# In attention, the scores of the next unit are multiplied ahead of the transposes of the last unit's probabilities

## Chip, cores and metric

The kernel runs on one core of one Trainium2 chip, in one launch. The metric is the device time of that launch in microseconds (us); smaller is better. The median of three runs before the change is 1122.41 us (1121.69 to 1124.14).

## The reference

One layer of an encoder trunk over 1024 tokens of width 1024, all in float32: a norm, one input projection whose columns feed a pooling mixer and attention, an output projection with residual, a gated MLP with a causal convolution, a gated per-layer embedding, and a final norm. The change lies in attention alone:

```python
q, k, v = jnp.split(z[..., POOL_W:], 3, axis=-1)     # 8 heads of 64
...
# chunk_attention: each chunk of 64 tokens attends to itself and the 8 chunks before it
s = jnp.einsum('bqhd,bkhd->bhqk', qb, kb) * scale + bias   # clipped relative position, per head
s = jnp.where(valid, s, -jnp.inf)
pr = jax.nn.softmax(s, axis=-1)
out = jnp.einsum('bhqk,bkhd->bqhd', pr, vb)
```

## The kernel before

The engines go by their short names: PE multiplies matrices, ACT and DVE work elementwise, POOL does a few elementwise pieces, SP issues transfers. Matrices are held as two parts, a high one rounded to float32r and a low one that holds the remainder, and a product is three matmuls (`mm3`, L136 to L138). So whatever is made elementwise and multiplied later is split by two instructions: a copy of the high part on ACT and a subtraction on DVE.

**Units.** The 1024 tokens are 8 query tiles of 128. Attention works on pairs of heads, `c` = 0 to 3, and in each on 6 units: unit 0 holds query tiles 0, 1 and 2, units 1 to 5 hold tiles 3 to 7, one each. There are 24 units (`NU`), and 25 visits `unit(u)`. A visit multiplies the scores of unit `u`, and takes the probabilities of unit `u - 1`, whose softmax was made in the visit before, one step on. A query tile looks at up to 5 key tiles (`BANDT`).

**A visit on PE.** PE's order is the order of the program (`manual_schedule`), and so is that of ACT and DVE in this stretch. In a visit, PE runs

- `probs_t(u - 1)` (L421): the probabilities of the last unit, two heads, are transposed by PE in pieces of 64 by 64, four per key tile of the unit, so 16 to 24 matmuls. The first 8 pieces of 64 columns go to banks 2 and 3 of PSUM (called near here), those of a fifth key tile and on to the last columns of banks 6 and 7 (far);
- `scores(u)` (L398): 12 matmuls for one query tile, 18 for unit 0 of a head pair. The two heads run side by side, each on 64 rows of the array. Head 0 writes bank 4, then 6, head 1 bank 5, then 7;
- matmuls of the projections that are still to be done (`fill`, a generator: q and k of the next head pairs, then the pooling mixer's columns), 12 to 27 of them, alternating between banks 0 and 1;
- in three of six visits, `values(u - 1)` (L473): the products of probabilities and v, for a group of query tiles (0 to 2, 3 to 5, or 6 and 7) whose last unit was just transposed. They go to bank 5 and the free one of banks 0 and 1, or, for the group of two tiles, both heads into one bank. ACT copies half of each result to `otmp` (L476) and DVE adds it to the other half (L479).

**A visit on ACT and DVE.** Their instructions are put into a list with due times (`push`) and issued in order of those when the visit calls `flush()`, which is after its projection matmuls have been issued. The list of a visit holds

- of the transposed probabilities: ACT's copies (L439) and DVE's remainders (L441), near ones ahead of far ones. The transposes of the next visit write the same banks again;
- of the softmax of the new scores: DVE adds the bias and takes the minimum (`least`, L363 for four and five key tiles, L367 for fewer), from PSUM to `Sb`; ACT's exponential with its sum (L375); DVE's reciprocal (L378); the scaling, by DVE for head 0 (L373) and by ACT for head 1 (L371). `Sb` has one buffer per head, which the transposes read;
- the copies of finished projections (L279 for q and k, L559 for the mixer) and the splits of q and k (L308 to L312) and of weights (L502, L504).

The lines of the change stand in `unit`, L671 and L673:

```python
            if u:
                probs_out(probs_t(u - 1), valued[0])
            if u < NU:
                softmax(scores(u), valued[0])
```

`probs_t` and `scores` issue PE's matmuls at once; `probs_out` and `softmax` only push ACT's and DVE's instructions.

Of the kernel before, what the change touches and what calls it, by code (L numbers as in the profile page):

```python
# [75 lines left out]
NU = len(UNITS)  # L76
# [8 lines left out]
def group_at(t):  # L85

    return next(g for g in GROUPS if g[0] <= t < g[1])


def is_last(u):  # L90

    t = UNITS[u][1][-1]
    return t + 1 == group_at(t)[1]
# [8 lines left out]
def trunk(tc, xT, pT, vecs, w_qk0, w_in, w_v, bias, counts, pool_w, w_out, w_up, w_down,  # L102
# [4 lines left out]
    with tc.tile_pool(name="sb", bufs=1) as sb, \  # L107
# [176 lines left out]
        def push(t, *fns):  # L284

            for n, fn in enumerate(fns):
                pending.append((t + 0.8 * n, len(pending), fn))

        def flush():
            todo = sorted(pending, key=lambda p: p[:2])  # L290
            pending.clear()
            owed.clear()
            for _, _, fn in todo:
                fn()
# [51 lines left out]
        def load_bias(h):  # L346
            b = biasb[h % 3]
            sp.dma_start(b, bias[h])

            def turned():  # L350
                act.activation(b, b, AF.Copy, scale=-1.0)
                pool.memset(b[0:64, 576:640], BIG)
                pool.memset(b[64:128, 0:64], BIG)
            return turned

        def softmax(todo, valued):

            for i, (x, b, ps, S, s_) in enumerate(todo):
                z = 2 * i / len(todo)

                def least(b=b, ps=ps, S=S, s_=s_):
                    if len(ps.shape) == 3:
                        dve.tensor_tensor_reduce(  # L363
                            S.rearrange("p (a b) -> p a b", a=2), ps,
                            b.rearrange("p (a b) -> p a b", a=2), 1.0, BIG, ALU.add, ALU.min, s_[:, 0:1])
                    else:
                        dve.tensor_tensor_reduce(S, ps, b, 1.0, BIG, ALU.add, ALU.min, s_[:, 0:1])  # L367

                def scaled(x=x, S=S, s_=s_):
                    if x:  # L370
                        act.activation(S, S, AF.Copy, scale=s_[:, 2:3])  # L371
                    else:
                        dve.tensor_scalar(S, S, s_[:, 2:3], None, ALU.mult)  # L373
                push(1.0 + 0.8 * z, least)
                push(1.9 + 0.85 * z, lambda S=S, s_=s_: act.activation(  # L375
                    S, S, AF.Exp, bias=s_[:, 0:1], scale=-1.0, accum_out=s_[:, 1:2]))
                ready = max(2.95 + 0.01 * z, 1.91 + 0.85 * z) if valued else 2.95 + 0.55 * z
                push(ready, lambda s_=s_: dve.reciprocal(s_[:, 2:3], s_[:, 1:2]))  # L378
                push(3.9 + 0.1 * z if x else max(ready + 0.005, 3.0 + (0.01 if valued else 0.55) * z), scaled)
# [4 lines left out]
        def scores(u):  # L384

            c, ts = UNITS[u]
            Kh, Kl = K[c % 2]
            todo = []
            for z, t in enumerate(ts):
                ki, nk = max(0, t - 4) * P, min(t + 1, BANDT)  # L390
                n = nk * P
                wide = n // 2 if nk > 3 else max(n, 256)
                off, place = (0, 1, 3)[z] * P, ((0, 0), (0, 256), (1, 0))[z]
                places = [[4 + x + 2 * (place[0] + y) for y in range(2 if nk > 3 else 1)] for x in range(2)]
                for i, (q, k) in enumerate(((Q[0], Kh), (Q[0], Kl), (Q[1], Kh))):
                    for y in range(len(places[0])):
                        for x in range(2):
                            pe.matmul(PS[:, places[x][y], place[1]:place[1] + wide], q[halves[x], t * P:(t + 1) * P],  # L398
                                      k[halves[x], ki + y * wide:ki + (y + 1) * wide], start=i == 0, stop=i == 2,
                                      tile_position=(HD * x, 0))  # L400
                for x in range(2):
                    p0 = places[x][0]
                    ps = PS[:, p0:p0 + 3:2, 0:wide] if nk > 3 else PS[:, p0, place[1]:place[1] + n]
                    todo.append((x, biasb[(2 * c + x) % 3][:, 640 - n:640], ps, Sb[x][:, off:off + n], st[nstat[0] % 8]))
                    nstat[0] += 1
            return todo

        def probs_t(u):

            c, ts = UNITS[u]  # L410
            total = key_tiles(u)

            def place(x, m):
                n = 2 * m + x
                return (2, HD * n) if n < 8 else (6, 512 + HD * (n - 2 * total))

            for x in range(2):
                for m in range(total):
                    bank, col = place(x, m)
                    for y in range(2):  # L420
                        pe.transpose(PS[:, bank + y, col:col + HD], Sb[x][halves[y], m * P:(m + 1) * P],  # L421
                                     ident[halves[y], halves[y]], tile_position=(HD * y, 0))
            todo, m = [], 0
            for t in ts:
                nk = min(t + 1, BANDT)
                b0 = block_at(t + 1 - nk, t)
                for a, b in ((0, min(nk, 4 - m)), (max(4 - m, 0), nk)):
                    if b > a:
                        bank, col = place(0, m + a)
                        todo.append((b0 + a, b0 + b, bank, PS[:, bank:bank + 2, col:col + 2 * HD * (b - a)]))  # L430
                m += nk
            return todo

        def probs_out(todo, valued):
            for a, b, bank, ps in todo:
                src = ps.rearrange("p a (n q) -> p n a q", q=HD)
                hi, lo = [pt[:, a:b].rearrange("p k x (a q) -> p (k x) a q", a=2) for pt in PT]
                far = bank > 3
                push(3.5 if far else 0.0, lambda hi=hi, src=src: act.activation(hi, src, AF.Copy))  # L439
                push((3.55 if valued else 4.4) if far else 2.5 if valued else 3.7,  # L440
                     lambda lo=lo, src=src, hi=hi: dve.tensor_tensor(lo, src, rv(hi), ALU.subtract))  # L441

        credit, turns, valued = 0.0, [], [False]
# [203 lines left out]
        def lay_due(u):  # L647

            for c, x, h in list(qk_ready):
                if u >= (c - 1) * PER + (0 if x else PER - 1 if h else 1):  # L650
                    qk_ready.remove((c, x, h))
                    push(max(4.8, now[0] + 0.4), *lay(c, x, h))
# [4 lines left out]
        def unit(u):  # L657

            nonlocal credit
            now[0] = 0.0  # L660
            unit_at[0] = u
            if u < NU:
                c, ts = UNITS[u]
                for h in range(2 if ts[-1] > 3 else 1):
                    while not all((c, x, h) in laid for x in range(2)):
                        next(fill)
                        lay_due(u - 1)
                        flush()
            valued[0] = u > 0 and is_last(u - 1)
            if u:  # L670
                probs_out(probs_t(u - 1), valued[0])  # L671
            if u < NU:
                softmax(scores(u), valued[0])  # L673
                if u % PER == PER - 1:
                    for h in (2 * c + 3, 2 * c + 4):
                        if h < N_HEADS:
                            push(3.0, lambda h=h: turns.append(load_bias(h)))
                lay_due(u)
                credit += ROOM[u % PER]
                now[0] = 1.25  # L680
                least = LEAST[u % PER] if u else 0
                while credit >= 1 or least > 0:
                    if valued[0] and credit < 2 and least < 1 and 4.7 < at[0] < 5.4:
                        break
                    now[0] += STEP
                    credit -= 1
                    least -= 1
                    if next(fill, True) is False:
                        break
                    lay_due(u)  # L690
            else:
                for _ in range(DRAIN):
                    now[0] += STEP
                    next(fill)
            flush()
            if u:
                values(u - 1)
            if turns and (u % PER == PER - 1 or u % PER == 1):
                turns.pop(0)()
            run_later(LATER)  # L700
# [765 lines left out]
```

## Time and profile before

| | before |
|---|---|
| median of 3 runs | 1122.41 us (1121.69 to 1124.14) |
| the profiled execution, its own time | 1122.08 us |
| its span, first to last instruction | 1120.3 us |
| TensorE clock granted (mean) | 0.998 |
| PE busy | 1108.7 us, 99% |
| DVE busy | 850.7 us, 76% |
| ACT busy | 581.7 us, 52% |
| POOL busy | 167.9 us, 15% |
| first scores in the trace | 74.3 us |
| last transposes in the trace | 248.7 to 250.2 us |

How to read it: the profiled execution is one run; its time holds the span and 1.8 us around it. Busy time of PE is the union of its matmuls, whose ends are modelled and which overlap in the pipeline, so a short pause between two matmuls can hide in it; starts of matmuls tell more than their ends. Lines such as L421 are lines of the kernel; a group that a helper issues has the helper's line. In rows of the timeline stand the start, the duration, engine, line, operation, tiles written and read, shapes, and the count of merged instructions; in brackets how long the engine had been idle and what released it.

### The profile page before, as it was taken

How to read it: one execution, taken by the hardware profiler on the slowest of the kernel's cores; microseconds unless marked ns; L12 is line 12 of the kernel's file. 1: busy time of each engine (PE TensorE's matmuls, PEld its weight loads, DVE VectorE, ACT ScalarE, POOL GpSimd, SP SyncE). 2: the span in 40 equal slices, each digit the busy share in tenths (PEclk: the TensorE clock that was granted, in tenths of full speed). 3: DMA queues.
4: the chain of work that ended last, by engine and by line, in shares of the span. 5: the costliest groups of instructions: out<-in, count | busy, mean ns of one | idle time of the engine just before them, and what ended most of it. 6: DMA issues, size and time to landing. Idle time of an engine off the chain costs nothing.

```text
span 1120.3 us, 15614 instructions
## 1 busy us (share of the span) xinstructions
PE 1108.7 (99%) x5674; PEld 921.3 (82%) x5674; DVE 850.7 (76%) x1438; ACT 581.7 (52%) x1006; POOL 167.9 (15%) x212
## 2 busy tenths in 40 slices
PE   9999999999999999999999999999999999999997
PEld 7888888888888888888888888888888888888887
DVE  7537777778578878887787878777877789986845
ACT  8336777765665545443443444344544444674634
POOL 0000101186013200220121012201120112000000
PEclk9999999999999999999999999999999999999999
DMA  8100111104600452764567456756575556420003
GB/s 308 50 1 20 62 43 39 51 16 136 197 29 1 109 155 95 164 156 140 150 160 168 133 160 151 172 138 160 142 174 145 137 156 140 132 94 20 1 34 117
DMA packets 64878, 124.83 MB, mean 111 GB/s; under 512 B 7329, under 2 KB 8737, under 8 KB 64801
## 3 DMA queue, kind: packets, MB, share of 16 engines
q1 hardware_dynamic: 50688, 98.33, 26.8%
q0 software_dynamic: 13824, 25.17, 14.2%
q8 instruction: 44, 0.72, 0.3%
q10 hardware_dynamic: 288, 0.33, 0.1%
q14 instruction: 34, 0.27, 0.1%
HBM read 109.13 MB, written 14.68 MB: 111 GB/s over the span
## 4 chain that ended last, share of the span: by engine, by line
PE 65%; DVE 3%; issue 2%; ACT 1%; POOL 1%; POOLq 0%; DVEq 0%; ACTq 0%
PE PS L136 21%; PE PS L137 21%; PE PS L138 21%; DVE R L142 1%; ACT R L141 1%; POOL TB L925 0%; POOL F L915 0%; DVE F L907 0%; DVE F L1191 0%; ACT TB L896 0%; PE PS L778 0%; POOL small L782 0%; ACT F L770 0%; DVE TB L918 0%; DVE TB L919 0%
## 5 line engine op out<-in xcount | busy, mean ns | idle before, releaser
L136 PE MATMUL PS<-R 128*128 128x512 f32 (+1 forms) x1088 | 422.2, 388 | 0.2
L137 PE MATMUL PS<-R 128*128 128x512 f32 (+1 forms) x1088 | 418.7, 385 | 0.0
L138 PE MATMUL PS<-R 128*128 128x512 f32 (+1 forms) x1088 | 418.5, 385 | 0.0
L136 PEld LDWEIGHTS PS<-R 128*128 128x128 f32 x1088 | 204.6, 188 | 44.6 <-issue 2.9
L138 PEld LDWEIGHTS PS<-R 128*128 128x128 f32 x1088 | 204.5, 188 | 41.3
L137 PEld LDWEIGHTS PS<-R 128*128 128x128 f32 x1088 | 204.6, 188 | 39.8 <-DVE R L249 0.2
L141 ACT ACTIVATE R<-F 128x512 fp32r<-128x512 f32 (+2 forms) x221 | 137.4, 636 | 177.1 <-PE PS L137 85.6
L142 DVE TENSOR_TENSOR R<-F,R 128x512 fp32r<-128x512 f32 (+2 forms) x221 | 154.5, 713 | 49.7 <-ACT R L141 49.0
L1160 DVE TENSOR_TENSOR F<-F,PS 128x512 f32<-128x512 f32 x140 | 92.6, 681 | 6.8 <-PE PS L138 6.5
L850 DVE TENSOR_TENSOR F<-F 128x512 f32<-128x512 f32 x88 | 60.5, 688 | 44.8 <-DMA F<-in_w_up 42.1
L141 ACT ACTIVATE BQ<-RW 128x512 fp32r<-128x512 f32 x90 | 52.6, 622 | 80.4 <-PE PS L137 76.3
L1103 POOL DMA_DIRECT2D RW<-Yd x56 | 49.5, 889 | 264.4 <-DMA RW<-Yd 200.8
L1103 POOL DMA_DIRECT2D RW<-in_w_down x40 | 36.5, 966 | 228.7 <-DMA RW<-in_w_down 191.1
L142 DVE TENSOR_TENSOR BQ<-RW,BQ 128x512 fp32r<-128x512 f32 x90 | 59.1, 684 | 2.6 <-PE PS L137 2.2
L137 PE MATMUL PS<-BQ 128*128 128x512 f32 x140 | 54.6, 390 | 0.1
L136 PE MATMUL PS<-R,BQ 128*128 128x512 f32 x140 | 54.5, 389 | 0.0
L138 PE MATMUL PS<-R,BQ 128*128 128x512 f32 x140 | 54.5, 389 | 0.0
L136 PE MATMUL PS<-BQ 128*128 128x512 f32 x140 | 54.5, 389 | 0.0
L137 PE MATMUL PS<-R,BQ 128*128 128x512 f32 x140 | 54.5, 389 | 0.0
L138 PE MATMUL PS<-BQ 128*128 128x512 f32 x140 | 54.5, 389 | 0.0
L986 ACT ACTIVATE F<-F,vec 128x1024 f32<-128x1024 f32 (+1 forms) x25 | 28.6, 1143 | 44.1 <-DVE F L961 41.9
L375 ACT ACTIVATE F<-F,small 128x640 f32<-128x640 f32 (+4 forms) x64 | 44.0, 689 | 14.0 <-DVE small L363 12.6
(177 smaller groups left out, 1589.7 us busy)
## 6 DMA issues: line engine op xcount, KB each, us to landing
F<-in_w_up SPq DMA_DIRECT2D x91, 256.0 KB, 4.3
RW<-Yd SPq DMA_DIRECT2D x60, 256.0 KB, 3.8
RW<-Yd POOLq DMA_DIRECT2D x56, 256.0 KB, 4.9
RW<-in_w_down SPq DMA_DIRECT2D x50, 256.0 KB, 2.9
RW<-in_w_down POOLq DMA_DIRECT2D x40, 256.0 KB, 6.6
Yd<-F SPq DMA_DIRECT2D x40, 256.0 KB, 3.1
F<-in_w_in SPq DMA_DIRECT2D x10, 512.0 KB, 3.5
F<-in_xT SPq DMA_DIRECT2D x16, 256.0 KB, 5.4
```

The costliest lines, as they stand in the source:

```text
L136: pe.matmul(ps, ahi, bhi, start=first, stop=False, skip_group_check=more)
L137: pe.matmul(ps, ahi, blo, start=False, stop=False, skip_group_check=more)
L138: pe.matmul(ps, alo, bhi, start=False, stop=last, skip_group_check=more)
L141: both = (act.activation(hi, src, AF.Copy), dve.tensor_tensor(lo, src, rv(hi), ALU.subtract))
L142: dve.tensor_tensor(lo, src, rv(hi), ALU.subtract))
L375: push(1.9 + 0.85 * z, lambda S=S, s_=s_: act.activation(S, S, AF.Exp, bias=s_[:, 0:1], scale=-1.0, accum_out=s_[:, 1:2]))
L850: return dve.tensor_tensor(rawu[to], rawu[a], rawu[b], op)
L986: act.activation(y, Gb[:, 2 + a:2 + b], AF.Identity, bias=vec[:, C_CB + fi:C_CB + fi + 1], scale=cw(2))
L1103: pool.dma_start(t, src, accum_op=ALU.add)
L1160: dve.tensor_tensor(t, t, PS[:, 4 + d], ALU.subtract if n in (1, 5) else ALU.add)
```

## The change

In a visit, `scores(u)` is called, and so its matmuls are issued on PE, before `probs_t(u - 1)`; the list of scores is handed to `softmax` afterwards. The calls of `push` keep their order and their due times, so that the order of ACT's and DVE's instructions is the same.

```diff
             valued[0] = u > 0 and is_last(u - 1)
+            todo = scores(u) if u < NU else []
             if u:
                 probs_out(probs_t(u - 1), valued[0])
             if u < NU:
-                softmax(scores(u), valued[0])
+                softmax(todo, valued[0])
                 if u % PER == PER - 1:
```

Visit 0 has no probabilities to transpose and visit 24 no scores to multiply; the order on PE changes in the other 23.

## The prediction

> **What bounds the kernel now.** I read the page first: its part 1 shows TensorE (PE) at 99% of the span, so time moves only where PE stands still or where its own instructions take longer.
>
> ```profile
> span 1120.3 us, 15614 instructions
> PE   1108.7 (99%) x5674; PEld 921.3 (82%) x5674; DVE 850.7 (76%) x1438; ACT 581.7 (52%) x1006; POOL 167.9 (15%) x212
> ```
>
> Then the windows view of attention, 80 to 256 us, and PE's waits there (who waited for whom: total, times, longest).
>
> ```profile
> 80.00:256.00 176.00, 172.85 (x1416) 144.30 (x1416) 131.51 (x318) 125.33 (x258) 45.44 (x67) 1.00 0.14 42
> ...
> PE PS L473 <- DVE B L441: 1.8, 4, 0.8
> PE PS L421 <- DVE B L441: 0.8, 2, 0.5
> PE PS L473 <- ACT B L439: 0.5, 1, 0.5
> ```
>
> PE is idle 176.00 - 172.85 = 3.15 us there, and only 0.8 of it stands ahead of the transposes (L421), where the scores could go first. So there is little to win; what the change can cost must be looked for in one visit. The timeline of one whole visit (start, duration):
>
> ```profile
> 98.01 1.53 DVE L441 TENSOR_TENSOR B<-PS,B 128x1024 fp32r<-128x1024 f32 x2
> ...
> 99.19 0.39 PE L138 MATMUL PS<-R 128*128 128x512 f32 x1
> ...
> 99.51 0.84 PE L421 MATMUL PS<-ident,F 64*128 64x64 f32 x20
> ...
> 100.16 1.13 PE L398 MATMUL PS<-R 64*128 64x320 f32 x12
> 100.33 1.03 ACT L439 ACTIVATE B<-PS 128x1024 fp32r<-128x1024 f32 x1 [0.84 <-PE PS L421]
> ...
> 101.22 0.50 PE L136 MATMUL PS<-R,B 128*128 128x512 f32 x1
> 101.32 0.82 DVE L363 CUSTOM_DVE_ANT_0 F<-PS,F 128x640 f32<-128x640 f32 x1 [1.77 <-PE PS L398]
> ...
> 102.19 0.83 ACT L375 ACTIVATE F<-F,small 128x640 f32<-128x640 f32 x1 [0.83 <-DVE small L363]
> ...
> 103.83 0.36 ACT L439 ACTIVATE B<-PS 128x256 fp32r<-128x256 f32 x1
> ...
> 104.06 1.33 PE L473 MATMUL PS<-B,R 128*128 128x384 f32 x7
> ...
> 105.20 0.42 DVE L441 TENSOR_TENSOR B<-PS,B 128x256 fp32r<-128x256 f32 x1
> ...
> 105.68 0.55 PE L473 MATMUL PS<-B,R 128*128 128x128 f32 x2 [0.29 <-DVE B L441]
> ```
>
> Read it thus. Transposes T (L421) run 99.51 to 100.16, scores S (L398) to 101.22, then projection matmuls, then the values V (L473). ACT copies what T made, first the near part (1024 wide, banks 2 and 3), starting 0.17 after T's end; DVE starts its minimum over the scores (L363) 0.10 after S's end; the exponential (L375) starts 0.05 after that minimum. V stops at its eighth matmul until DVE's far remainder (105.20 + 0.42 = 105.62) is there: 105.68, 0.06 later.
>
> **The change part by part.** Nothing is added or removed; in 23 visits (units 1 to 23) 12 or 18 score matmuls with their weight loads pass 16 to 24 transposes on PE. No DMA is issued by the moved step, and no order written out for ACT or DVE changes; SP's and POOL's queues are not passed.
>
> *Borders between kinds of matmul.* A projection to T costs 99.51 - 99.19 = 0.32. The other borders:
>
> ```profile
> 73.96 0.39 PE L138 MATMUL PS<-B,R 128*128 128x512 f32 x1
> 74.28 1.50 PE L398 MATMUL PS<-R 64*128 64x256 f32 x18
> 75.71 0.50 PE L136 MATMUL PS<-R 128*128 128x512 f32 x1
> ...
> 205.34 0.84 PE L421 MATMUL PS<-ident,F 64*128 64x64 f32 x20
> 205.99 1.48 PE L398 MATMUL PS<-R 64*128 64x256 f32 x18
> 207.40 0.50 PE L136 MATMUL PS<-R 128*128 128x512 f32 x1
> ...
> 249.65 0.59 PE L421 MATMUL PS<-ident,F 64*128 64x64 f32 x12 [0.46 <-DVE B L441]
> 250.17 0.50 PE L136 MATMUL PS<-R 128*128 128x512 f32 x1
> ```
>
> A projection to S costs the same 0.32 (74.28 - 73.96). Eighteen scores take 1.43 behind a projection and 1.41 behind T: +0.02. T costs 0.65 / 20 = 0.033 each ahead of S, so 12 would be 0.39; ahead of a projection they took 0.52: +0.13 at most. S, no longer ahead of a projection, gives something back, which no row of before shows: between nothing and twice that 0.11 net (0.22). Per visit -0.09 to +0.13, over 23 visits -2.1 to +3.0 us. I take **0**: the same three borders (wide to narrow, narrow to narrow, narrow to wide) stand in every visit, only the names differ.
>
> *A. The wait that is new.* V of the group of query tiles 0 to 2 puts its first half in bank 5; S writes bank 5 with its second matmul. Before, T stood between.
>
> ```profile
> 131.79 0.55 DVE L479 TENSOR_TENSOR F<-PS,F 64x384 f32<-64x384 f32 x1 [0.34 <-ACT F L476]
> 131.94 0.71 PE L421 MATMUL PS<-ident,F 64*128 64x64 f32 x16
> ```
>
> S would start at 131.94, but DVE reads bank 5 until 132.34; with 0.06 to pass it on, 0.46 of wait. The second pair's weights load meanwhile, so that it can follow closer than the 0.18 that a pair takes on average (1.06 / 6); I put 0.1 on that: 0.35 a time, in 4 head pairs **+1.4** (1.3, or 1.8 with nothing given back). This is late next on PE, and what queues behind it is T, and so the near copies.
>
> *How finely waits are told apart.* S writes banks 4 to 7; T's far part lies at the end of banks 6 and 7, in other columns. Does a wait go by bank or by column? Two rows of a V whose halves share one bank:
>
> ```profile
> 124.45 0.77 ACT L476 ACTIVATE F<-PS 64x256 f32<-64x256 f32 x2 [1.27 <-PE PS L473]
> ...
> 125.25 0.42 DVE L479 TENSOR_TENSOR F<-PS,F 64x256 f32<-64x256 f32 x1 [2.92 <-ACT F L476]
> ```
>
> DVE's first add needs only the first of these two ACT copies, done by half of 0.77, yet it starts after the second (125.22), which reads other columns of the same bank. With two banks (131.79) it starts right behind its own. So I take: by bank. Then the minimum over new scores (banks 4 to 7) starts only when T's far part is written, which by the visit's row is 0.19 after T's end (99.51 + 0.84 = 100.35 against 100.16), and 0.03 to pass it on, as S now does (100.16 + 1.13 = 101.29, DVE at 101.32): X + 0.21, X being where the projections start, against X + 0.10 now. The Trainium skill, page "PSUM — Partial Sum Buffer", section "PSUM bank collisions raise a hardware error", says to guard PSUM by bank and quadrant and not by address; the two rows agree, and the rule speaks against this change, for it makes two orders out of one: by it the sum is the +2.6 below, without it +1.4.
>
> *C. The softmax behind.* The near copy moves from T's end 1.06 ahead of X to X itself: it runs X + 0.17 to X + 1.20, and the exponentials start there instead of at X + 0.97 (102.19): 0.2 later. DVE's run up to the far remainder starts 0.11 later and is unbroken, so V's eighth matmul comes 0.11 later. Two visits like this one, and two more with V ending on that remainder, 0.1 each: **+0.45**. In the visits without V this delay is covered, as T itself comes 1.06 later.
>
> *B. One visit pays more.* Where unit 18 (three tiles at once) is scored, from 205.34 above:
>
> ```profile
> 206.16 1.03 ACT L439 ACTIVATE B<-PS 128x1024 fp32r<-128x1024 f32 x1 [0.21 <-PE PS L421]
> 207.41 0.40 ACT L375 ACTIVATE F<-F,small 128x128 f32<-128x128 f32 x1 [0.22 <-DVE small L367]
> ...
> 210.38 0.36 ACT L439 ACTIVATE B<-PS 128x256 fp32r<-128x256 f32 x1
> ...
> 210.94 3.12 PE L473 MATMUL PS<-B,R 128*128 128x256 f32 x24
> ```
>
> The near copy would start at 207.40 + 0.17, so six exponentials (210.38 - 207.41 = 2.97) run 208.60 to 211.57 and the far copy ends at 211.93. V needs that at its fourth matmul, as the same V shows one head pair earlier:
>
> ```profile
> 119.92 0.51 PE L473 MATMUL PS<-B,R 128*128 128x256 f32 x3
> ...
> 120.97 0.96 PE L473 MATMUL PS<-B,R 128*128 128x128 f32 x6 [0.55 <-ACT B L439]
> ```
>
> Three matmuls take about 0.34 (24 take 3.12 by the row above, the short ones among them first), so the fourth would start at 211.28. The wait is 0.7, of which a later wait of this V takes 0.1: **+0.6**. Units 6 and 12 have ACT busy anyway, or 24 projection matmuls to cover it.
>
> *D. Scores held by the far remainder.* By bank, the second pair of S (0.23 into S) waits for DVE's far remainder of the visit before, which ended at 98.01 + 1.53 = 99.54; 0.2 later and 0.06 on, 99.80, against 99.51 + 0.23 = 99.74: 0.06. Three such, and one late one worth 0.17: **+0.35**.
>
> *E. The gain.* In one visit T waits:
>
> ```profile
> 157.77 1.54 DVE L441 TENSOR_TENSOR B<-PS,B 128x1024 fp32r<-128x1024 f32 x2
> ...
> 158.33 0.39 PE L138 MATMUL PS<-R,B 128*128 128x512 f32 x1
> ...
> 159.04 0.92 PE L421 MATMUL PS<-ident,F 64*128 64x64 f32 x20 [0.33 <-DVE B L441]
> ```
>
> T starts 0.71 behind the last projection instead of 0.32, and loses another 0.06 inside. The 18 scores go ahead here and touch banks 6 and 7 only in their last 0.5 us, so this is won: **-0.45**. *F.* The last T (248.7 to 250.2) has no scores left to go ahead and waits for the same DVE chain, 0.2 later: **+0.2**.
>
> Sum: 0 + 1.4 + 0.45 + 0.6 + 0.35 - 0.45 + 0.2 = 2.55, say **+2.6 us**. It is made against the profiled run's 1122.08 us (span 1120.3), which stands 0.33 under the median of 1122.41; I put it on the median: **1125.0 us**. What a measurement can tell from no change is about 0.2%, 2.2 us; this is on its edge.
>
> **The rivals.**
> *1, waits go by column.* Then D falls away, the minimum of the first head starts when its own transposes are read, about X - 0.1, and the two V of C come 0.2 earlier each: 1.4 - 0.4 + 0.6 - 0.45 + 0.2 = +1.4, 1123.8 us. Against it: the row at 125.25.
> *2, dearer borders.* All of +0.13 per visit, nothing given back: +3.0 on top, 1128.0 us. For it: 250.17; against it: the wide-to-narrow borders cost the same.
> *3, not slower: cheaper borders.* S hidden between projection and T gives back 0.2, so that each visit gains 0.09: 2.6 - 2.1 = +0.5, 1122.9 us. It breaks even at 0.11 per visit and would be measurably faster from 0.21. No row shows such a border; S in two row halves ends with long matmuls that T must wait for.
>
> **How the numbers follow.** Forecast (by bank, 0 for borders; own range 1123.8 to 1126.6): 0.50, of which 0.30 lies over +2.2 us. Rival 1: 0.18. Rival 2: 0.12. Rival 3: 0.10, of which 0.02 faster. Something else: 0.10 (0.04 faster, 0.02 same, 0.04 slower). Faster 0.06, same 0.20 + 0.18 + 0.08 + 0.02 = 0.48, slower 0.30 + 0.12 + 0.04 = 0.46. The range takes in rivals 2 and 3 to their ends: 1121.5 to 1128.0.
>
> **What would show it.** After: S directly behind the 0.32 border and T at its end in 23 visits; the same S + T time of 1.71; in four visits S with one step of 0.4 behind V, released by L479; near copies starting 0.17 after T's end; L363 starting after T's end (bank) or before it (column, rival 1); unit 18's V stopped by L439 for about 0.7; no wait ahead of T near 159. The prediction is wrong if S + T differs from 1.71 by over 0.05 in every visit, or if V in other visits starts to wait for L439.

## Result and profile after

| | before | changed |
|---|---|---|
| median of 22 runs each, same chip | 1122.51 us | 1124.33 us |
| profiled execution's span | 1120.3 us | 1122.5 us |
| PE busy | 1108.7 us | 1110.6 us |
| first scores to the projection behind the last values | 184.96 us | 186.59 us |

The ratio is 1.0016, 95% interval 1.001 to 1.0022: slower by 1.8 us, a little less than the 0.2% named as the edge, with an interval that leaves out 1. The last row of the table is the stretch in which the order changed; it is read from starts of PE rows (74.28 to 259.24 before, 74.77 to 261.36 after) and grew by 1.63 us. Another 0.5 us of the span's difference lies ahead of the first scores, where the two kernels issue the same instructions; in the traces of the experiments below that point lies between 74.05 and 75.42, whatever the edit.

First the page, then the windows view and PE's waits in attention, as shown of before:

```profile
span 1122.5 us, 15614 instructions
...
PE 1110.6 (99%) x5674; PEld 923.8 (82%) x5674; DVE 851.7 (76%) x1438; ACT 579.1 (52%) x1006; POOL 166.6 (15%) x212
```

```profile
80.50:258.20 177.70, 174.56 (x1416) 147.46 (x1416) 131.38 (x317) 123.08 (x258) 45.68 (x68) 1.00 0.13 43
```

```profile
PE PS L473 <- DVE B L441: 1.8, 4, 0.7
PE PS L473 <- ACT B L439: 0.8, 2, 0.5
PE PS L421 <- DVE B L441: 0.5, 1, 0.5
```

PE is idle 177.70 - 174.56 = 3.14 us where it was 3.15. The idle time did not grow, though the stretch did: the new loss hides in PE's busy time, because a matmul that runs in one half of the array's rows keeps the engine busy in this view while the other half stands still. The waits view shows only two small exchanges: 0.3 less for the transposes (the one visit that was to gain) and 0.3 more for the values waiting for ACT (the one visit that was to pay). So the answer must come from starts of blocks; a block is a run of PE's rows of one kind, such as the 12 score matmuls of a visit. The same ordinary visit in the timeline of the changed kernel:

```profile
100.07 0.39 PE L138 MATMUL PS<-R 128*128 128x512 f32 x1
100.39 1.15 PE L398 MATMUL PS<-R 64*128 64x320 f32 x12
101.37 0.78 PE L421 MATMUL PS<-ident,F 64*128 64x64 f32 x20
102.09 0.50 PE L136 MATMUL PS<-R,B 128*128 128x512 f32 x1
...
104.94 1.31 PE L473 MATMUL PS<-B,R 128*128 128x384 f32 x7
```

```profile
102.13 1.03 ACT L439 ACTIVATE B<-PS 128x1024 fp32r<-128x1024 f32 x1 [1.76 <-PE PS L421]
102.19 0.82 DVE L363 CUSTOM_DVE_ANT_0 F<-PS,F 128x640 f32<-128x640 f32 x1 [1.75 <-PE PS L421]
...
103.06 0.83 ACT L375 ACTIVATE F<-F,small 128x640 f32<-128x640 f32 x1
...
106.08 0.42 DVE L441 TENSOR_TENSOR B<-PS,B 128x256 fp32r<-128x256 f32 x1
```

Scores and transposes take 102.09 - 100.39 = 1.70, as before (1.71): nothing is gained or lost by the order itself. The minimum starts 0.10 behind the start of the projections, as before; the exponential 0.97 behind it, as before. This visit costs the same. One of the four visits behind the values of query tiles 0 to 2 does not. Its rows before, and then after:

```profile
87.61 0.71 PE L421 MATMUL PS<-ident,F 64*128 64x64 f32 x16
88.14 1.13 PE L398 MATMUL PS<-R 64*128 64x320 f32 x12
89.19 0.51 PE L136 MATMUL PS<-R 128*128 128x512 f32 x1
```

```profile
86.76 1.39 PE L473 MATMUL PS<-B,R 128*128 128x384 f32 x9
88.08 1.55 PE L398 MATMUL PS<-R 64*128 64x320 f32 x12
89.34 0.79 PE L421 MATMUL PS<-ident,F 64*128 64x64 f32 x16
90.06 0.50 PE L136 MATMUL PS<-R 128*128 128x512 f32 x1
```

```profile
87.89 0.55 DVE L479 TENSOR_TENSOR F<-PS,F 64x384 f32<-64x384 f32 x1 [0.47 <-ACT F L476]
...
89.92 0.82 DVE L363 CUSTOM_DVE_ANT_0 F<-PS,F 128x640 f32<-128x640 f32 x1 [0.65 <-PE PS L421]
```

The scores start at 88.08 behind the values, DVE reads bank 5 until 87.89 + 0.55 = 88.44, and the pair of blocks ends at 90.06: 1.98, where the same visit took 1.58 before (87.61 to 89.19). PE's rows are not broken, since the first score, for head 0 and bank 4, runs until the second one starts; no wait is listed. The four such visits lose 0.40, 0.42, 0.41 and 0.43.

The visit that was to gain, and the values that were to pay:

```profile
159.70 0.39 PE L138 MATMUL PS<-R,B 128*128 128x512 f32 x1
160.02 1.51 PE L398 MATMUL PS<-R 64*128 64x256 f32 x18
161.36 0.79 PE L421 MATMUL PS<-ident,F 64*128 64x64 f32 x20
162.07 0.50 PE L136 MATMUL PS<-R 128*128 128x512 f32 x1
```

```profile
212.24 0.51 PE L473 MATMUL PS<-B,R 128*128 128x256 f32 x3
213.05 2.72 PE L473 MATMUL PS<-B,R 128*128 128x128 f32 x21 [0.30 <-ACT B L439]
```

In the first, the scores follow the projections by the usual 0.32 and the transposes wait for nothing. The second stops at its fourth matmul for ACT's far copy.

The whole of the stretch, summed from starts of blocks: scores with transposes in the four visits behind the values of query tiles 0 to 2, +1.65; the values at 212.24, +0.41; the visit at 160, with the projections ahead of it, -0.44; all other blocks together +0.01. The sum is 1.63.

### The profile page after: what moved, and what is told of

It reads as the page before. It is cut to its first block, busy times and chain, and to the rows that moved or that the text cites. A ratio compares the mean times of both kernels' runs of the same rounds, so it can differ in the third digit from the quotient of the medians.

```text
span 1122.5 us, 15614 instructions
## 1 busy us (share of the span) xinstructions
PE 1110.6 (99%) x5674; PEld 923.8 (82%) x5674; DVE 851.7 (76%) x1438; ACT 579.1 (52%) x1006; POOL 166.6 (15%) x212
## 4 chain that ended last, share of the span: by engine, by line
PE 64%; DVE 3%; issue 2%; ACT 1%; POOL 1%; POOLq 0%; DVEq 0%; ACTq 0%
PE PS L136 21%; PE PS L138 21%; PE PS L137 21%; DVE R L142 1%; ACT R L141 1%; POOL TB L926 0%; POOL F L916 0%; DVE F L1192 0%; DVE F L908 0%; ACT TB L897 0%; PE PS L779 0%; POOL small L783 0%; ACT F L771 0%; DVE TB L919 0%; DVE TB L920 0%
## 5 line engine op out<-in xcount | busy, mean ns | idle before, releaser
L439 ACT ACTIVATE B<-PS 128x256 fp32r<-128x256 f32 (+2 forms) x52 | 33.2, 658 | 24.0 <-PE PS L421 24.0
```

## The experiments

Two theories stood against each other. Theory W: the loss is PE waiting for DVE's read of bank 5, in four visits. Theory R: the loss is spread over all 23 visits, because the copies of the transposed pieces start later. The medians below each stand beside the kernel before in the same session (1122.6, 1122.49 or 1122.5 us); the stretch is the one of the table.

**The bank of the first half changed.**

```diff
-                Os = [PS[:, bank, 0:n * P] for bank in (5, free)]
+                Os = [PS[:, bank, 0:n * P] for bank in (5 if t0 else 2, free)]
```

> The changed kernel, but the first half of the values of query tiles 0 to 2 goes to bank 2 instead of bank 5. Theory W (the loss is PE waiting for DVE's read of bank 5 in four visits, 0.41 each): the four scores that follow take 0.98 instead of 1.25 to 1.27 and the transposes behind them 0.59 instead of 0.73, 1.65 us off the changed kernel: about 1122.7 us, level with before. Theory R (the loss is spread over the 23 visits, because copies of the transposed pieces start later): the time stays near 1124.3 us.

Measured: 1122.9 us, ratio 1.0000 (0.9991 to 1.0009); stretch 185.05 us, 1.54 less than the changed kernel.

```profile
88.27 1.14 PE L398 MATMUL PS<-R 64*128 64x320 f32 x12
89.25 0.66 PE L421 MATMUL PS<-ident,F 64*128 64x64 f32 x16
89.84 0.50 PE L136 MATMUL PS<-R 128*128 128x512 f32 x1
```

In PE's timeline of this kernel the scores take 0.98 and the 16 transposes 0.59 (0.72 in the changed kernel), 1.57 together: the whole of the 0.41 is gone in each of the four visits. The transposes had been late too, because they alternate between the two row halves and one of these was still behind with its scores. Nothing else in the kernel was touched: this is what theory W said.

**The order changed in those four visits alone, and in all but those.**

```diff
+            ahead = u < NU and u % PER == 2        # in the second kernel: !=
+            todo = scores(u) if ahead else []
...
-                softmax(todo, valued[0])
+                softmax(todo if ahead else scores(u), valued[0])
```

> Scores go first in the four visits alone that follow the values of query tiles 0 to 2; the other visits keep the old order. Theory W: nearly all of the loss is here, +1.65 us against before (1124.2). Theory R: four of 23 visits carry four 23rds of the loss, +0.3 us (1122.8).

Measured: 1124.34 us, ratio 1.0013 (1.0004 to 1.0022), stretch 186.81. That is 1.85 over before: 1.65 in the four visits, and most of the rest behind the last of them, where the next transposes wait for DVE's remainder (0.24 more).

> Scores go first in every visit but those four. Theory W: level with before within 0.1 us (one visit gains 0.44 where the transposes waited, one loses 0.41 in the values): 1122.5. Theory R: 19 of 23 parts of the loss stay, +1.5 us (1124.0).

Measured: 1122.68 us, ratio 0.9998 (0.9989 to 1.0007), stretch 184.97. Four visits carry the loss. The nineteen others carry none on balance: in them the gain of 0.44 and the 0.41 of the values cancel. Theory R is out.

**The wait made longer.**

```diff
+                Os = [PS[:, bank, 0:n * P] for bank in ((5, free) if t0 else (free, 5))]
```

> The changed kernel with the two banks of the values of query tiles 0 to 2 exchanged, so that bank 5 holds the second half, which DVE reads last (its add ends 1.19 after the values' end instead of 0.36). Theory W: the step in the four scores grows from 0.41 to about 1.25, +3.3 us on the changed kernel: 1127.6. Theory R: no change, 1124.3.

Measured: 1127.3 us, ratio 1.0041 (1.0028 to 1.0053); stretch 189.91, 3.3 over the changed kernel. PE's waits, and its timeline and DVE's in the first of the visits:

```profile
PE PS L398 <- DVE F L479: 3.3, 4, 0.8
...
88.47 0.41 PE L398 MATMUL PS<-R 64*128 64x320 f32 x1
89.70 1.14 PE L398 MATMUL PS<-R 64*128 64x320 f32 x11 [0.83 <-DVE F L479]
```

```profile
89.09 0.56 DVE L479 TENSOR_TENSOR F<-PS,F 64x384 f32<-64x384 f32 x1 [0.27 <-ACT F L476]
```

Now the wait is long enough to be listed. The second score starts at 89.70, 0.05 behind the end of DVE's add (89.65), 1.23 behind the first. Of these 1.23 only 0.83 is listed as idle time, the part behind the end of the first score (88.47 + 0.41). The step moves with DVE's read of bank 5.

**By bank or by column: the far pieces first.**

```diff
-            for x in range(2):
-                for m in range(total):
...
+            for x, m in sorted(((x, m) for x in range(2) for m in range(total)),
+                               key=lambda p: 2 * p[1] + p[0] < 8):
...
```

> The changed kernel with the far pieces (banks 6 and 7) transposed first in each visit, then the near ones. If DVE's minimum over the new scores waits for the far pieces because they share banks 6 and 7 with the scores (waits by bank), it starts as soon as the first head's pieces are read, about 0.2 us ahead of now (at X - 0.1 instead of X + 0.10, X the start of the projections), and the two values that wait 0.46 for DVE's far remainder (104.9 and 196.4) start their eighth matmul about 0.2 earlier: -0.4 us, which the time cannot tell but the trace can. If it waits for the whole of the transposes for another reason, both stay as they are.

Measured: 1123.54 us, ratio 1.0008 (0.9999 to 1.0017), stretch 186.31. The two values blocks took 4.02 and 4.00 instead of 4.25 and 4.24. The timeline (its lines stand one higher, L420 for L421):

```profile
101.07 0.78 PE L420 MATMUL PS<-ident,F 64*128 64x64 f32 x20
101.64 0.82 DVE L363 CUSTOM_DVE_ANT_0 F<-PS,F 128x640 f32<-128x640 f32 x1 [1.48 <-PE PS L420]
101.78 0.50 PE L136 MATMUL PS<-R,B 128*128 128x512 f32 x1
```

The minimum starts 0.14 ahead of the projections instead of 0.10 behind them: with the pieces for banks 6 and 7 written early, only the reads of the first head's probabilities hold it. The changed kernel shows the same by itself at 89.92 above, in a visit whose transposes have no far piece: 0.14 ahead of 90.06. So the waits of this program go by bank. The Trainium skill's page "PSUM — Partial Sum Buffer", section "PSUM bank collisions raise a hardware error", asks for a guard by bank and quadrant, with by bank as the simple version, and not by address; these rows agree with it.

**The values' own waits.** Independent of the change, most waits that PE had left (1.8 and 0.8 in the list of the changed kernel) were those of the values for the far copy and its remainder. Here both are issued earlier.

```diff
-                push(3.5 if far else 0.0, lambda hi=hi, src=src: ...)
-                push((3.55 if valued else 4.4) if far else ...
+                push((2.0 if valued else 3.5) if far else 0.0, lambda hi=hi, src=src: ...)
+                push((2.55 if valued else 4.4) if far else ...
```

> The changed kernel, and in the visits that multiply values ACT's far copy is due behind the first exponential (2.0 instead of 3.5) and DVE's far remainder directly behind the near one (2.55 instead of 3.55). If the values' waits are a matter of order on ACT and DVE, they fall: 0.4 each at 104.9 and 196.4, 0.46 at 212.2, 1.3 at 120.8, 0.9 at 220.9, together about 3.3 us: 1121.0. If ACT and DVE are simply full in those visits, the waits move to the next transposes and the time stays at 1124.3.

Measured: 1123.31 us, ratio 1.0006 (0.9997 to 1.0015), stretch 185.67: only 0.9 of the 3.3 expected. The values did fall, from 37.10 to 32.99 us in all. But two visits with the bank 5 wait grew from 2.0 to 2.96 and 3.10, and one block of projections from 5.57 to 6.30. PE's waits name the first of these, and the timelines of PE and DVE show it (the wait for L371 stands behind the longer projections):

```profile
PE PS L398 <- DVE F L479: 2.1, 2, 1.1
PE PS L473 <- ACT F L371: 0.6, 1, 0.6
PE PS L421 <- DVE B L441: 0.5, 1, 0.5
```

```profile
131.04 0.41 PE L398 MATMUL PS<-R 64*128 64x320 f32 x1
132.43 0.56 PE L398 MATMUL PS<-R 64*128 64x320 f32 x4 [0.98 <-DVE F L479]
```

```profile
131.82 1.14 DVE L479 TENSOR_TENSOR F<-PS,F 64x384 f32<-64x384 f32 x2 [0.34 <-ACT F L476]
```

The values now end while ACT is still at other work (its splits, until 131.3), so the copy and the add that free bank 5 come later behind them, and the scores that the change put there wait for it.

Next, bank 2 and the early far pieces together:

> Bank 2 for the values of query tiles 0 to 2 and the far pieces early, on the changed order: 1.65 and 3.3 us off the changed kernel, 1119.4 us, if the two add up.

Measured: 1120.27 us, ratio 0.9981 (0.9973 to 0.9990), stretch 182.71. With bank 2 those two visits take 2.03 and 2.18, not 2.96 and 3.10. They are not back at 1.57, for now the transposes, which write bank 2, wait for L479:

```profile
130.79 1.14 PE L398 MATMUL PS<-R 64*128 64x320 f32 x12
132.18 0.71 PE L421 MATMUL PS<-ident,F 64*128 64x64 f32 x16 [0.25 <-DVE F L479]
```

And the old order with bank 5 and the far pieces early:

> The old order with the far pieces early. Same waits in the values but for the one at 212.2 (0.15 here): about 3.0 us off before, 1119.5 us. Against the kernel with both this tells whether the changed order has a worth of its own once its bank wait is gone: it should be 0.44 (the one visit whose transposes waited), under what the times can tell.

Measured: 1120.56 us, ratio 0.9984 (0.9975 to 0.9992), stretch 182.90. Less came than expected from both. In the old order the scores of those two visits wait for L479 and bank 5, though 16 transposes stand ahead of them: the visits take 2.47 and 2.37 where they took 1.58. With the changed order and bank 2 the transposes wait, as shown, and one block of projections still takes 6.30. DVE's timeline of that kernel gave the cause of the longer projections:

```profile
161.80 0.56 DVE L367 CUSTOM_DVE_ANT_0 F<-PS,F 128x384 f32<-128x384 f32 x1 [0.80 <-ACT B L439]
```

**The far copy behind the minima.** In both kernels with early far pieces, where a unit of three tiles is scored:

```diff
-                push((2.0 if valued else 3.5) if far else 0.0, ...
+                push((2.4 if key_tiles(unit_at[0]) == 6 else 2.0 if valued else 3.5) if far else 0.0, ...
```

> The kernel with both edits (bank 2, far pieces early, changed order), but where a unit of three tiles is scored ACT's far copy is due at 2.4, behind the minima that read banks 6 and 7. In the kernel with both, DVE's minimum waited 0.80 at 161.8 for that copy, which reads other columns of the same banks, and the values behind it began 0.7 late. If a wait goes by bank even between two reads, that stretch of projections falls from 6.30 back to 5.57 and the time by 0.7: about 1119.6 us. If the delay came from elsewhere: 1120.3.

Measured: 1119.31 us, ratio 0.9972 (0.9962 to 0.9983), stretch 182.04. DVE's timeline, same place:

```profile
160.76 0.55 DVE L367 CUSTOM_DVE_ANT_0 F<-PS,F 128x384 f32<-128x384 f32 x1
```

The wait of 0.80 is gone and the projections take 5.57 again: DVE had waited for an ACT read of other columns of the banks it was to read. In this program two reads of a bank wait for each other too.

The same two due times on the old order with bank 5:

> The same two due times on the order of before and with bank 5 as before. Whether the changed order has a worth of its own beside them: it saves the one wait of transposes (0.44) and loses nothing that these edits leave, so this kernel should be 0.4 to 0.7 us slower than the one with the changed order and bank 2, about 1120.3 us; equal times would say that the order is worth nothing that a run can tell.

Measured: 1120.71 us, ratio 0.9988 (0.9979 to 0.9997), stretch 183.29. The kernel with the changed order and bank 2 is 1.4 us faster than this one, more than expected. PE's waits for L479 in that kernel, and then in this one:

```profile
PE PS L421 <- DVE F L479: 0.5, 2, 0.4
```

```profile
PE PS L398 <- DVE F L479: 1.0, 2, 0.6
```

The stretches differ by 1.25: 0.44 from the transposes that no longer wait, and 0.42 and 0.43 in two visits where the old order, with bank 5, waits longer for L479. Only the 0.44 belongs to the order alone. The other two come from order and bank together: in both kernels the block that runs second waits for the read, and it starts behind 16 transposes (0.52) in the one and behind 12 scores (0.98) in the other. The old order with bank 2 was not run, so what the order is worth with that bank stays open. The kernel with the changed order, bank 2 and the new due times is 3.2 us faster than the one before (1119.31 against 1122.5).

## Why the prediction was right or wrong

The forecast was +2.6 us (1125.0); measured were +1.8, inside its own range of 1123.8 to 1126.6 and within the 0.2% called the same, which had a chance of 0.48. Point by point:

- *Borders, 0*: right. Scores with transposes take 1.70 after 1.71, 2.06 after 2.06. Rivals 2 and 3 are out.
- *A, +1.4*: the mechanism and the place were right, shown by four experiments; it measured 1.65, within its 1.3 to 1.8. The nearness is partly luck, since two slips cancel in part: the read ends 0.36 behind the start of the scores (88.44 against 88.08) and not 0.40, which makes the wait 0.41 and not 0.46; and nothing of it is given back, where 0.1 was booked, for the transposes are held up by the late row half as well.
- *By bank*: right, shown by the far pieces put first; rival 1 is out, though its number (1123.8) lies a little nearer to the measured one than the forecast's. That is luck: it leaves out D, which measured nothing, for a reason that the runs do not bear out, and books a gain of 0.4 for C's values that did not come.
- *E, -0.45*: right, -0.44.
- *B, +0.6*: right in place, measured +0.41. *C, +0.45*, *D, +0.35* and *F, +0.2* measured nothing: the values of two visits like C's first one took 4.25 and 4.24 after 4.25 and 4.25, no visit's scores waited for a far remainder, and the last transposes took what they took before.

So the sum was 0.9 too high (2.55 against the 1.62 below), and B, C, D and F share the step that failed: the place of the transposes' end. The prediction put the near copy 0.17 and the minimum 0.21 behind the start of the projections. They came 0.04 and 0.10 behind it (102.13 and 102.19 against 102.09). It had itself read that 12 transposes take 0.13 longer ahead of a projection, and booked that as time in the border, but it did not move their last matmul forward by it: the border stands behind the last transpose, not ahead of the first. Before, the border behind the scores lay there in the same way. With the minimum where it was before, DVE's chain starts as it did, and C, D and F vanish.

B hangs on ACT, and there a second step adds to the first. The prediction let the exponentials start at the end of the near copy. In the visit that scores unit 18, whose projections start at 208.71, ACT's timeline shows:

```profile
208.76 1.03 ACT L439 ACTIVATE B<-PS 128x1024 fp32r<-128x1024 f32 x1 [1.49 <-PE PS L421]
209.68 0.39 ACT L375 ACTIVATE F<-F,small 128x128 f32<-128x128 f32 x1
```

The copy ends at 209.79 by this view, and the exponential starts 0.11 ahead of that: 0.97 behind the projections, where the prediction had 1.20. That takes 0.23 off B's 0.6; 0.41 was measured.

The remaining cost is then 1.65 + 0.41 - 0.44 = 1.62 us, as the traces have it.

## What to carry to other kernels

When two blocks on one engine change places, list for each bank who reads it last and when: the block that moves up loses the cover that the other gave it, and a wait may then arise in a place where none was listed before. Price each consumer from the last matmul that feeds it and not from the start of the next block; at a border between kinds of matmul the two differ. Before dropping such a change, see whether another bank is free at that moment: here that turned a loss into nothing. Most of what was gained beyond that came from the earlier copies, which gained 1.8 to 1.9 us on the old order too.

## What the runs showed of the hardware that was not expected

A wait of one row half of the array shows as idle time of PE only from the end of the matmul that runs in the other half: four waits of 0.41 left the idle time of the stretch at 3.14 us against 3.15, and only starts of blocks showed them, while with bank 5 second the waits of 1.23 showed as 0.83 each. ACT's next instruction started 0.11 us ahead of the end that the profile gives to the one before it (209.68 against 209.79). DVE's read waited 0.80 us for an ACT read of other columns of the same banks in one place (161.80), as a write waits for a read. These are waits that the program carries; no run leaves one out, so what would happen without them is not shown.
